# A hybrid attention block on one core: output projection reachable from attention's tail, first q and k by halves, shared transfer time in the planner

## The chip, the core and the metric

The kernel runs on one NeuronCore of a Trainium2 chip. TensorE (PE in the profile) multiplies into PSUM; VectorE (DVE), ScalarE (ACT) and GpSimd (POOL) work elementwise, and the queue of SyncE (SP) issues nearly all transfers. The engines run side by side; each takes its own instructions strictly in the order in which they were written. The metric is the device time of one execution in microseconds (us); lower is better. Before: 1434.74 us, the median of three runs (1434.43 to 1435.29).

## The reference

One layer over 1024 tokens of width 1024, all float32, each sub-layer between RMS norms with a residual:

- Token mixing: one projection of the normed input gives q, k and v of 16 heads of 64. Eight heads are "fox" heads: causal softmax attention with a cumulated log forget gate as bias. Eight are "chunk" heads: attention over the own chunk of 64 and the eight before it, with a relative-position bias. Each group's output is RMS-normed over its 512 columns, the two are joined, and `y @ w_out` follows (the output projection).
- Cross-attention of four heads of 256 into 256 memory tokens: projections `w_mq`, `w_mk`, `w_mv`, `w_mo`.
- An MLP of hidden size 4096 with a squared ReLU.

## The kernel before

**Arithmetic.** A product in float32 is made of three faster ones: each operand is split into a high and a low part (`hi`, `lo`), and `mm3` (lines 195 to 197) adds hi·hi, hi·lo and lo·hi in one PSUM bank. A weight block of 128x1024 comes by a transfer into one of three `wraw` buffers, ACT writes its high part (line 499), DVE or POOL its low part (line 505), and then the buffer is free for the next block. For q, k and v the block is also scaled: ACT sums its squares (line 462), PE adds them over the partitions (`nq`, line 472), POOL scales, ACT and POOL split.

**Stages.** A prologue written by hand norms the input and makes v of the first heads. The attention phase follows, up to about 517 us of the trace: for eight pairs of heads (chunk pairs 0 and 1, fox pairs 0 to 3, chunk pairs 2 and 3) the projections q and k (and v from the fifth pair on), scores (`sc..g` for chunk, `sf..g` for fox heads, two banks), softmax by DVE, ACT and POOL, transposes of the probabilities (`ptr`, line 795, split into `phl` by ACT, line 805, and DVE, lines 801 and 803), and products with v (`pv`, lines 840 to 843, read out into `o`, which goes to memory tensors `od`). Beside them run the memory projections `mk` and `mv`. The second phase holds the output projection `yw` (four 512x512 quarters for each of two head groups g = 0, 1; quarters by the half th of the tokens and the half nh of the columns), the queries of the cross-attention (`mq`), that attention itself (`ms`, `mtr`, `mo`), and its output projection (`ym`). From about 840 us on the MLP follows, written by hand.

**What sets the order.** In the attention phase and the second phase a planner, the class `Flow`, writes the instructions. It steps through generators ("streams"); each step of a stream is a few matmuls with a cost and a condition, and at every moment the first stream in the list whose condition holds places its step on PE. The last stream of the list is the filler: projections that need nothing of the attention chain (`filler_steps` in the attention phase, `second_filler` in the second). Work for DVE, ACT, POOL and the transfer queue is put into lists (`flow.put`, `flow.load`) with a planned earliest time, a cost and a level; when the planned engine is free, the entry of the lowest level that may start is written next. A transfer's result is planned to be there a fixed time after its issue. All these times are the planner's own; on the chip only the resulting order and the data count.

**Around the end of attention.** `Outputs` loads the finished fox-head outputs back (`oin`), four blocks for each half th of the tokens; ACT scales them into `yT_hi`, DVE writes `yT_lo`, ACT squares them (line 1146), DVE adds the squares up into `sq` (line 1124), and PE sums `sq` over the partitions (`ssh`, line 1164), which gives the norm factor `rs` of that half. The first `yw` matmul of the second phase needs `yT` and `rs` of half 0 and the first two blocks of `w_out`. The blocks of `w_out` come through the same three `wraw` buffers, behind the eight blocks of `w_mv`. In the profile's names `whiwo` and `whimv` are high parts of such blocks; `vm_hi` and `vm_lo` read the `mv` products out of PSUM.

The planner's list of the attention phase ends with the rows

```
flow.run([scale_steps(), value_steps(), turn_steps(), score_steps(), side_steps(), rstd_steps(0),
          filler_steps(keep)])
```

Of the kernel before, what the change touches and what calls it, by code (L numbers as in the profile page):

```python
# [20 lines left out]
ALU = mybir.AluOpType  # L21
# [36 lines left out]
class Flow:  # L58
# [4 lines left out]
    def __init__(self):  # L63
        self.now = self.end = 0.0
# [12 lines left out]
    def load(self, at, call, then=None, took=4.5, level=0):  # L77
        self.put("D", at, 0.55, call, then and (lambda end: then(end + took)), level)
# [59 lines left out]
def build(ctx, tc, nc, out, t):  # L138
# [265 lines left out]
    class Stock:  # L404
# [126 lines left out]
        def pump(self):  # L531

            while self.to_load:
# [13 lines left out]
                flow.put("D", flow.now, 0.55, lambda: None, lambda at, k=key: seen.__setitem__(("raw", k), at + 4.2))  # L547
# [37 lines left out]
    def split(key, at):  # L585
# [9 lines left out]
        flow.put("G", at, 1.15, lambda: stock.scale(key), lambda end: flow.put("S", end, 1.06, lambda: stock.hi(key), low, 2), 2)  # L595
# [44 lines left out]
    class Biases:  # L640
# [5 lines left out]
        def pump(self):  # L646
            while self.left and free["bias"].ready():
# [245 lines left out]
    def project_steps(what, n, part):  # L893
# [7 lines left out]
        for th in range(2):  # L901
# [31 lines left out]
            for a, (own, oth) in enumerate(HALVES):  # L933
# [14 lines left out]
                else:  # L948
# [16 lines left out]
    def side_steps():  # L965
# [24 lines left out]
        for k in range(0, KC, 2):  # L990
# [17 lines left out]
            flow.put("S", flow.end, 0.6, lambda src=src, dh=dh: nc.scalar.activation(dh, src, AF.Copy), lo, 1)  # L1008
# [89 lines left out]
    class Outputs:  # L1098
# [182 lines left out]
    def norm_steps():  # L1281
# [9 lines left out]
        def scales():  # L1291
# [9 lines left out]
            ("G", 0.7, lambda: nc.gpsimd.tensor_tensor(sw1, sw1, mhalf[:, 0:1], op=ALU.pow)), ("V", 1.1, scales)])))  # L1301
# [97 lines left out]
    def close_row(nm, n, at, dst, gnext, then):  # L1399
# [1712 lines left out]
```

## Time and profile before

| | before |
|---|---|
| median of 3 runs | 1434.74 us |
| the profiled execution, its own time | 1436.12 us |
| its span, first to last instruction | 1434.3 us |
| PE, DVE, ACT, POOL busy | 98%, 81%, 69%, 32% |
| granted TensorE clock, mean over the span | 0.994 |
| transfers | 295.72 MB, mean 206 GB/s |

Busy shares are means over stages. PE is busy nearly always, so the places that count are the few where PE stands still or runs at a lower clock. Three views tell them: the list of waits gives who ended PE's idle times, the timeline of an engine gives each instruction with the idle time before it in brackets, and the table by stretches gives the granted clock (PEclk, 1.00 is full speed). A matmul's printed duration is longer than its share of PE's time, since matmuls overlap; the distance from start to start is what one costs.

### The profile page before, as it was taken

The page shows a single profiled execution, that of the slowest core. Times are in us where ns is not written, and L with a number is a line of the kernel's source. Part 1 is how long each engine was busy: PE and PEld are TensorE (multiplying, and loading weights), DVE is VectorE, ACT ScalarE, POOL GpSimd, SP SyncE. Part 2 cuts the span into 40 slices and gives each one's busy share as a digit, 9 for nine tenths or more (in the row PEclk, how much of TensorE's full clock was granted, in tenths as well). Part 3 has the DMA queues.
Part 4 walks back from the last instruction along what each step waited for, and adds up shares of the span by engine and source line. Part 5 has one row for each costly group of instructions (what it writes and reads, how often), then busy time and mean ns, then how long its engine had stood idle before and what let it go on. Part 6 is the DMA issues. An engine that isn't in the chain of part 4 may idle for free.

```text
span 1434.3 us, 22534 instructions
## 1 busy us (share of the span) xinstructions
PE 1400.8 (98%) x7681; PEld 922.4 (64%) x7681; DVE 1156.0 (81%) x1863; ACT 989.1 (69%) x1688; POOL 454.8 (32%) x615
## 2 busy tenths in 40 slices
PE   8999999999999989999999999999999999999998
PEld 8746666666668868887888864444444445666653
DVE  7888776867777863779887978677998987899998
ACT  6678878888778844798465645786776657665654
POOL 2467768787645400121021531002223100000003
PEclk9999999999999989999999999999999999999999
DMA  7143465445436677471314656976888998686885
GB/s 281 49 132 91 142 187 170 121 148 142 128 106 167 203 223 275 169 292 38 111 59 133 205 177 220 339 256 219 290 287 290 347 366 306 235 307 225 308 304 205
DMA packets 118802, 295.72 MB, mean 206 GB/s; under 512 B 13448, under 2 KB 31888, under 8 KB 118688
## 3 DMA queue, kind: packets, MB, share of 16 engines
q1 hardware_dynamic: 118544, 294.03, 61.3%
q8 instruction: 60, 0.98, 0.3%
q14 instruction: 54, 0.44, 0.1%
q10 hardware_dynamic: 144, 0.26, 0.1%
HBM read 220.26 MB, written 65.59 MB: 199 GB/s over the span
## 4 chain that ended last, share of the span: by engine, by line
PE 71%; DVE 11%; ACT 6%; issue 5%; DMA 3%; POOL 2%; SPq 0%; DVEq 0%; ACTq 0%; POOLq 0%
PE ptr L795 4%; PE fx L195 3%; PE fx L196 3%; PE fx L197 3%; PE yw L195 2%; PE yw L196 2%; PE yw L197 2%; PE pv L840 2%; PE mq L196 2%; PE mq L197 2%; PE mq L195 2%; PE px L197 2%; PE px L196 2%; PE px L195 2%; PE k L195 1%
## 5 line engine op out<-in xcount | busy, mean ns | idle before, releaser
L805 ACT ACTIVATE phl<-ptr 128x512 f16<-128x512 f32 (+3 forms) x152 | 80.4, 537 | 41.3 <-PE ptr L795 39.5
L2879 POOL TENSOR_SCALAR rf<-sf 128x1 f32<-128x1 f32 x7 | 5.8, 825 | 280.3 <-ACT jf L2858 280.0
L2574 POOL TENSOR_TENSOR sc<-wf,wf 128x512 f32<-128x512 f32 x8 | 11.2, 1398 | 173.0 <-DMA wf<-in_w_ff 109.2
L1734 POOL TENSOR_SCALAR mp<-mp,mst 128x256 f32<-128x256 f32 x32 | 22.6, 709 | 127.0 <-DVE mst L1733 104.1
L803 DVE TENSOR_TENSOR phl<-ptr,phl 128x384 fp32r<-128x384 f32 (+1 forms) x76 | 46.3, 616 | 19.2 <-ACT phl L805 18.6
L801 DVE SCALAR_TENSOR_TENSOR phl<-ptr,phl 128x384 f16<-128x384 f32 (+1 forms) x76 | 46.4, 616 | 16.5 <-ACT phl L805 15.5
L840 PE MATMUL pv<-phl,vs 128*128 128x512 f32 (+1 forms) x152 | 53.0, 431 | 1.0 <-DVE phl L803 1.0
L2723 ACT ACTIVATE vhif<-ra,fsc 128x1024 f16<-128x1024 f32 x34 | 38.9, 1143 | 20.8 <-PE fx L197 12.6
L2725 DVE SCALAR_TENSOR_TENSOR vhif<-ra,fsc,vhif 128x1024 f16<-128x1024 f32 x34 | 43.5, 1279 | 11.2 <-ACT vhif L2723 10.9
L2723 ACT ACTIVATE whif<-ra,fsc 128x1024 f16<-128x1024 f32 x34 | 38.8, 1142 | 19.3 <-PE fx L197 10.3
L195 PE MATMUL yw<-whiwo,yT_hi 128*128 128x512 f32 x128 | 51.8, 404 | 0.0
L196 PE MATMUL yw<-wlowo,yT_hi 128*128 128x512 f32 x128 | 51.1, 399 | 0.0
L197 PE MATMUL yw<-whiwo,yT_lo 128*128 128x512 f32 x128 | 51.0, 399 | 0.0
L196 PE MATMUL q<-hF_lo,wq 128*128 128x512 f16 x128 | 48.5, 379 | 1.8 <-DVE hF_lo L2235 1.8
L195 PE MATMUL fx<-vlof,vhif 128*128 128x512 f16 x128 | 48.5, 379 | 0.8 <-DVE yc L2930 0.8
L195 PE MATMUL k<-hF_hi,wk 128*128 128x512 f16 x128 | 49.2, 384 | 0.0
L195 PE MATMUL q<-hF_hi,wq 128*128 128x512 f16 x128 | 48.9, 382 | 0.0
L196 PE MATMUL k<-hF_lo,wk 128*128 128x512 f16 x128 | 48.8, 381 | 0.0
L2725 DVE SCALAR_TENSOR_TENSOR whif<-ra,fsc,whif 128x1024 f16<-128x1024 f32 x34 | 43.5, 1279 | 6.5 <-ACT whif L2723 6.4
L197 PE MATMUL k<-hF_hi,wk 128*128 128x512 f16 x128 | 48.6, 380 | 0.0
L197 PE MATMUL q<-hF_hi,wq 128*128 128x512 f16 x128 | 48.5, 379 | 0.0
L195 PE MATMUL fx<-wlof,whif 128*128 128x512 f16 x128 | 48.5, 379 | 0.0
(855 smaller groups left out, 5350.5 us busy)
## 6 DMA issues: line engine op xcount, KB each, us to landing
wg<-in_w_ff SPq DMA_DIRECT2D x48, 512.0 KB, 5.3
ra<-gd SPq DMA_DIRECT2D x40, 512.0 KB, 4.8
wf<-in_w_ff SPq DMA_DIRECT2D x38, 512.0 KB, 4.5
wn<-in_w_ff SPq DMA_DIRECT2D x32, 512.0 KB, 4.8
w2n<-in_w_ff SPq DMA_DIRECT2D x32, 512.0 KB, 6.5
wi<-in_w_ff2q SPq DMA_DIRECT2D x28, 512.0 KB, 5.6
gd<-s SPq DMA_DIRECT2D x32, 256.0 KB, 6.0
gd<-g SPq DMA_DIRECT2D x19, 256.0 KB, 4.5
```

Source lines behind the costliest of these rows:

```text
L195: nc.tensor.matmul(ps, lh, rh, start=start, stop=False, skip_group_check=more)
L196: nc.tensor.matmul(ps, lh, rl, start=False, stop=False, skip_group_check=more)
L197: nc.tensor.matmul(ps, ll, rh, start=False, stop=stop, skip_group_check=more)
L795: nc.tensor.transpose(tr[:, m, :], sp[:, k * P:(k + 1) * P], ident)
L801: flow.put("V", at, 0.75, lambda: nc.vector.scalar_tensor_tensor(pl[:, live, :], tr[:, live, :], 2.0 ** 14, ph[:, live, :], op0=ALU.mult, ...
L803: if ph.dtype == F16 else nc.vector.tensor_sub(pl[:, live, :], tr[:, live, :], f(ph[:, live, :])), done)
L805: flow.put("S", flow.end, 0.6, lambda ph=ph, tr=tr, live=live: nc.scalar.activation(ph[:, live, :], tr[:, live, :], AF.Copy, scale=2.0 ** ...
L840: nc.tensor.matmul(pv[:, :, qs_, :], v, hl[:, :, hs, :], start=c == 0 and turn == 0, stop=last)
L1734: mul = lambda st=st, pr=pr: nc.gpsimd.tensor_scalar(pr, pr, st[:, 2:3], 1.0, op0=ALU.mult, op1=ALU.mult)
L2574: eng.tensor_sub(sc[:, k1], r0[:, k0], r1[:, k0])
L2723: nc.scalar.activation(ah, ra, AF.Copy, scale=su)
L2725: nc.vector.scalar_tensor_tensor(al, ra, su, ah, op0=ALU.mult, op1=ALU.subtract)
```

## The change

No instruction is added or removed in what is computed; the order changes from the first projections to the end of the second phase, and some transfers start elsewhere. The MLP's part is the same. Five edits:

1. **The output projection's stream is built before the attention phase** and given to its planner run as a stream after all others (`last=tail`); the run still ends when the other streams are empty, and the second phase goes on with the same stream.
2. **`Outputs` loads half 0 of the fox outputs once all q, k and v projections are placed** (and nine u4 buffers are free) instead of once all scores are placed; half 1 waits for the scores as before.
3. **The first pair's projections go by halves of the tokens**: q of half 0, k of half 0, q of half 1, k of half 1, where it was q, q, k, k.
4. **The planner counts shared transfer time**: `land` adds up the bytes at 310 KB a planned us, and a load is planned to be there at the later of its fixed time and the end of that sum. The copies between partitions of k are counted at 3.6 instead of 2.3.
5. **Other levels** for some 25 entries (an example is shown), and other starts and paces of three background streams: sums of squares of MLP weights (`Norms`: start 80 instead of 60; in the second phase three spare buffers instead of four), differences of query weights (`QuerySums`: start 100, pace 12 instead of 20, 18).

```diff
-        self.put("D", at, 0.55, call, then and (lambda end: then(end + took)), level)
+        self.put("D", at, 0.55, call, lambda end: self.land(end, took, then), level)
+
+    def land(self, end, took, then):
+        size = {2.2: 64, 2.5: 256, 3: 512, 3.5: 256, 3.6: 128, 4.2: 512, 4.5: 512, 6.0: 256, 7.5: 256}[took]
+        self.moved = max(self.moved, end + 1.5) + size / 310.0
+        if then:
+            then(max(end + took, self.moved + 0.6))
...
-    def run(self, streams, more=lambda: False):
-        heads = [[g, next(g, None)] for g in streams]
-        idle = 0
-        while any(h[1] for h in heads) or more():
+    def run(self, streams, more=lambda: False, last=None):
+        heads = [g if isinstance(g, list) else [g, next(g, None)] for g in streams]
+        needed, idle = list(heads), 0
+        if last:
+            heads.append(last)
+        while any(h[1] for h in needed) or more():
...
-                "G", end, 1.3, lambda: stock.lo(key, nc.gpsimd, 1), last, 2), 2)
+                "G", end, 1.3, lambda: stock.lo(key, nc.gpsimd, 1), last, 1), 2)
...
-                if not (there(("od", g), "scored") and free["u4"].ready(7) and (g == 0 or ("w", 1) in ys)):
+                late = there("scored")
+                if not (there(("od", g), "scored" if th or g else "projected") and
+                        free["u4"].ready(7 if late else 9) and (g == 0 or ("w", 1) in ys)):
...
-        START, PACE = 20.0, 18.0
+        START, PACE = 100.0, 12.0
...
             part = all_of(("qk", n), 12)
+            if n == 0:
+                for th in range(2):
+                    for what in "qk":
+                        yield from project_steps(what, n, part, (th,))
+                continue
...
+        seen["projected"] = flow.end
         yield from memory_steps(keep)
+
+    steps = second_filler()
+    tail = [steps, next(steps)]
...
-                  filler_steps(keep)])
+                  filler_steps(keep)], last=tail)
...
-                  norm_steps(), second_filler()], lambda: stock.to_load or stock.to_split)
+                  norm_steps(), tail], lambda: stock.to_load or stock.to_split)
```

How this moves instructions is shown at three places; numbers behind a name tell its instances apart, and in the changed file line numbers stand 9 to 12 higher.

**ACT at the end of attention.** Before (`whiwo_0_0`, `whiwo_0_1`: the two blocks of the first column half; `whiwo_1_0`: the first block of the second column half; `rs_6784`: norm factor of half 0):

```order
L1143 ACTIVATE yT_hi_6516<-oin_6521,gcol 128x512 x2
L1146 ACTIVATE oin_6520<-oin_6520 128x512
L1146 ACTIVATE oin_6521<-oin_6521 128x512 x2
L499 ACTIVATE whiwo_0_0_6808<-wrawwo_0_0_6752 128x1024
L499 ACTIVATE whiwo_1_0_6895<-wrawwo_1_0_6775 128x1024
L1086 ACTIVATE vm_hi_6572<-mv_6718 128x512
L499 ACTIVATE whiwo_0_1_6825<-wrawwo_0_1_6773 128x1024
L1086 ACTIVATE vm_hi_6573<-mv_6736 128x512
L1235 ACTIVATE wn_6811,wsq<-wn_6811 128x1024
L1458 ACTIVATE yw_6868<-yw_6867,rs_6784 128x512
```

With the change:

```order
L1155 ACTIVATE yT_hi_6579<-oin_6584,gcol 128x512
L1158 ACTIVATE oin_6584<-oin_6584 128x512 x2
L1096 ACTIVATE vm_hi_6471<-mv_6681 128x512
L508 ACTIVATE whiwo_0_1_6807<-wrawwo_0_1_6679 128x1024
L870 ACTIVATE o_6815<-pv_6764,wus 64x256
L1096 ACTIVATE vm_hi_6472<-mv_6692 128x512
L1470 ACTIVATE yw_6817<-yw_6816,rs_6555 128x512
L1247 ACTIVATE wn_6828,wsq<-wn_6828 128x1024
L508 ACTIVATE whiwo_1_0_6901<-wrawwo_1_0_6730 128x1024
L1470 ACTIVATE yw_6818<-yw_6849,rs_6555 128x512
```

`whiwo_1_0` stood ahead of both `vm_hi` and of `whiwo_0_1`; it now stands behind the first read-out of `yw`. `whiwo_0_0` stands nine rows above the first one shown.

**PE at the same place.** Before, the last `mv` matmuls, then the sum for half 1 (`ssh_6832`), then the output projection:

```order
L197 MATMUL mv_6736<-whimv_3_6748,mT_lo_5564 128x512
L1164 MATMUL ssh_6832<-o_81,sq_6519 128x1 x4
L1274 MATMUL top<-ident,wsq 128x128
L195 MATMUL yw_6867<-whiwo_0_0_6808,yT_hi_6508 128x512
L196 MATMUL yw_6867<-wlowo_0_0_6809,yT_hi_6508 128x512
```

With the change (the sum for half 0 stands 187 rows above):

```order
L206 MATMUL mv_6692<-whimv_3_6699,mT_lo_5470 128x512
L851 MATMUL pv_6764<-phl_6776,vs_71_5323 128x256
L204 MATMUL yw_6816<-whiwo_0_0_6715,yT_hi_5741 128x512
L204 MATMUL yw_6816<-whiwo_0_1_6807,yT_hi_5742 128x512
L205 MATMUL yw_6816<-wlowo_0_1_6808,yT_hi_5742 128x512
L206 MATMUL yw_6849<-whiwo_0_0_6715,yT_lo_5743 128x512
L1176 MATMUL ssh_6855<-o_81,sq_6582 128x1 x4
L1286 MATMUL top<-ident,wsq 128x128
```

Rows between these that differ in one name alone are left out: 15 `yw` matmuls now stand ahead of the sum for half 1. The last product of the attention stands right before them, where 42 `mv` matmuls had stood behind it.

**PE in chunk pair 1 (about 170 us of the trace).** Before, from one transpose group (`ptr_2134`) to the product that reads its split copy (`phl_2135`):

```order
L795 MATMUL ptr_2134<-ident,spc2g_1941 128x128
L840 MATMUL pv_2148<-phl_2105,vs_1_196 128x512
L840 MATMUL pv_2148<-phl_2105,vs_1_196 128x2x128
L795 MATMUL ptr_2154<-ident,spc2g_1941 128x128
L721 MATMUL sc3g_2165<-kd_1250,qs_1123 128x384
L722 MATMUL sc3g_2165<-kl_1251,qs_1123 128x384
L721 MATMUL sc3g_2168<-kd_1250,qs_1123 128x256
L722 MATMUL sc3g_2168<-kl_1251,qs_1123 128x256
L840 MATMUL pv_2148<-phl_2135,vs_2_197 128x512 x2
```

With the change, the same group (`ptr_2108`) and product (`phl_2109`):

```order
L804 MATMUL ptr_2108<-ident,spc2g_1888 128x128
L204 MATMUL q_1_2004<-hF_hi_699,wq_1191 128x512
L205 MATMUL q_1_2004<-hF_lo_701,wq_1191 128x512
L849 MATMUL pv_2128<-phl_2080,vs_1_196 128x512
L849 MATMUL pv_2128<-phl_2080,vs_1_196 128x2x128
L804 MATMUL ptr_2133<-ident,spc2g_1888 128x128
L730 MATMUL sc3g_2140<-kd_1232,qs_1115 128x384
L731 MATMUL sc3g_2140<-kl_1233,qs_1115 128x384
L730 MATMUL sc3g_2145<-kd_1232,qs_1115 128x256
L731 MATMUL sc3g_2145<-kl_1233,qs_1115 128x256
L849 MATMUL pv_2128<-phl_2109,vs_2_197 128x512 x2
```

Repeats are left out here too: the group's `ptr` rows are four, the next group's three, and six `q` matmuls (two `mm3`) now stand between the two groups, where none stood.

More of the change, by code (lines that the diff above doesn't have):

```diff
@@ L63, in __init__ @@
     def __init__(self):
-        self.now = self.end = 0.0
+        self.now = self.end = self.moved = 0.0
         self.free = dict.fromkeys(("V", "S", "G", "D"), 0.0)
@@ L546, in pump @@
                 self.load()
-                flow.put("D", flow.now, 0.55, lambda: None, lambda at, k=key: seen.__setitem__(("raw", k), at + 4.2))
+                flow.put("D", flow.now, 0.55, lambda: None, lambda at, k=key: flow.land(at, 4.2, mark(("raw", k))))
             while self.to_split and there(("raw", self.to_split[0])):
@@ L891, in all_of, with project_steps @@
         return one
-    def project_steps(what, n, part):
+    def project_steps(what, n, part, halves=range(2)):
         kind, pr = ORDER[n]
         u = 3 if what == "v" else 2
-        for th in range(2):
+        for th in halves:
             cs = slice(th * HT, (th + 1) * HT)
@@ L955, in then @@
                     def then(at, lo=lo, last=last, copy=copy, d=d, l=l):
-                        flow.load(at, lambda: copy(d), part, 2.3)
+                        flow.load(at, lambda: copy(d), part, 3.6)
                         flow.put("V", at, 0.75, lo, lambda end: (last(end), flow.load(
-                            end, lambda: copy(l), part, 2.3)), 1)
+                            end, lambda: copy(l), part, 3.6)), 1)
                     flow.put("S", flow.end, 0.7, hi, then, 1)
-        stock.done((what, n))
+        if 1 in halves:
+            stock.done((what, n))
     vt = {}
@@ L1006, in lo @@
                          lambda end: (free["tr"].give(end), seen.__setitem__(("mT", k), end)), 1)
[L1008 removed]
+            flow.put("S", flow.end, 0.6, lambda src=src, dh=dh: nc.scalar.activation(dh, src, AF.Copy), lo, 0)
         for _ in range(2):
@@ L1429, in wait @@
             if ("xt", nm, n) in seen:
-                flow.put("V", max(end, seen["xt", nm, n]), 1.3, add, store, 1)
+                flow.put("V", max(end, seen["xt", nm, n]), 1.3, add, store, 0)
             else:
                 flow.put("G", end + 0.5, 0.0, lambda: None, wait)
-        flow.put("G", at, 1.9, lambda: root(0, ss[:, 0:1], ss[:, 1:2]), wait, 1)
+        flow.put("G", at, 1.9, lambda: root(0, ss[:, 0:1], ss[:, 1:2]), wait, 0)
     def mix_steps(g):
@@ L1458, in mix_steps @@
                     flow.put("S", flow.end, 0.63, lambda yc=yc, ps=ps, r=r: nc.scalar.activation(
-                        yc, ps, AF.Copy, scale=r), free["mm"].give)
+                        yc, ps, AF.Copy, scale=r), free["mm"].give, 1)
                 else:
@@ L1467, in rest @@
                                   ("V", 0.7, lambda: nc.vector.tensor_tensor(yc, yc, gains["mix"][:, cs], op=ALU.mult))]
-                        flow.chain(at, parts_, (lambda end: close_row("w", n, end, x1d, "mem", mixed(n))) if nh else None, 1)
-                    flow.put("V", flow.end, 0.7, out, rest)
+                        flow.chain(at, parts_, (lambda end: close_row("w", n, end, x1d, "mem", mixed(n))) if nh else None, 5)
+                    flow.put("V", flow.end, 0.7, out, rest, 0)
             if th == 1:
@@ L1513, in lo @@
                     flow.put("V", at, 0.7, lambda: nc.vector.tensor_sub(dl, src, dh),
-                             lambda end: (free[bk].give(end), seen.__setitem__(key, end)))
-                flow.put("S", flow.end, 0.6, lambda src=src, dh=dh: nc.scalar.activation(dh, src, AF.Copy), lo)
+                             lambda end: (free[bk].give(end), seen.__setitem__(key, end)), 2)
+                flow.put("S", flow.end, 0.6, lambda src=src, dh=dh: nc.scalar.activation(dh, src, AF.Copy), lo, 2)
         for _ in range(4):
@@ L1622, in split @@
                          lambda at, hi=hi, lo=lo, r=raw[i], then=then: flow.put(
-                             "V", at, 1.22, lambda: nc.vector.tensor_sub(lo, r, f(hi)), then, 0), 0 if n == "A22" else 1)
+                             "V", at, 1.22, lambda: nc.vector.tensor_sub(lo, r, f(hi)), then, 0), 0 if n == "A22" else 3)
     class Finals:
@@ L1839, in operand_parts @@
                               ("V", 0.42, lambda: nc.vector.tensor_sub(s4, halves[0], L))],
-                   lambda at: (gone(at), [parts_of[n, k](at) for n in ("S2", "S1", "S4")]), 0)
+                   lambda at: (gone(at), [parts_of[n, k](at) for n in ("S2", "S1", "S4")]), 2)
         block(1, lambda at: (gone(at), lows[h, 1](at)), 1)
@@ L1869, in memory_out_steps @@
                                  "V", at, 0.7, lambda: nc.vector.tensor_sub(ol, ps, f(oh)),
-                                 lambda end: (free["pv"].give(end), done(end))))
+                                 lambda end: (free["pv"].give(end), done(end)), 3), 2)
                 free["pt"].give(flow.end)
@@ L1928, in gained @@
             return lambda at: flow.chain(at, parts_, (lambda e: close_row(
-                "m", b + 2 * th, e, x2d, "ff", mark(("h3", b + 2 * th)))) if close else None, 1)
+                "m", b + 2 * th, e, x2d, "ff", mark(("h3", b + 2 * th)))) if close else None, 3)
         def add(dst, x, then, op=nc.vector.tensor_add):
```

26 lines of the change are left out of this document (13 added, 13 removed).

## The prediction

> **What bounds the kernel now.** The page's head comes first: PE is busy for 98% of the span, so time can only come from the places where PE waits or runs slowly.
>
> ```profile
> span 1434.3 us, 22534 instructions
> PE 1400.8 (98%) x7681; PEld 922.4 (64%) x7681; DVE 1156.0 (81%) x1863; ACT 989.1 (69%) x1688; POOL 454.8 (32%) x615
> ```
>
> The list of waits (total us, times, longest) names the places; its longest single wait is at the end of attention:
>
> ```profile
> PE ssh L1164 <- DVE sq L1124: 5.7, 1, 5.7
> PE q L196 <- DVE hF_lo L2235: 1.8, 3, 0.8
> ```
>
> The timelines of SP, ACT, DVE and PE (start, duration, instruction, idle time before it and its releaser) say why:
>
> ```profile
> 512.59 0.38 SPq L450 DMA_DIRECT2D wrawwo<-in_w_out  x1
> 520.47 1.06 ACT L499 ACTIVATE whiwo<-wrawwo 128x1024 fp32r<-128x1024 f32 x1 [5.94 <-DMA wrawwo<-in_w_out]
> 521.44 0.58 ACT L1086 ACTIVATE vm_hi<-mv 128x512 fp32r<-128x512 f32 x1
> 521.91 1.05 ACT L499 ACTIVATE whiwo<-wrawwo 128x1024 fp32r<-128x1024 f32 x1
> 522.86 0.59 ACT L1086 ACTIVATE vm_hi<-mv 128x512 fp32r<-128x512 f32 x1
> 522.05 0.69 DVE L1087 TENSOR_TENSOR vm_lo<-mv,vm_hi 128x512 fp32r<-128x512 f32 x1 [5.76 <-ACT vm_hi L1086]
> 522.65 0.68 DVE L1124 TENSOR_TENSOR sq<-sq,oin 128x512 f32<-128x512 f32 x1
> 523.25 1.22 DVE L505 TENSOR_TENSOR wlowo<-wrawwo,whiwo 128x1024 fp32r<-128x1024 f32 x1
> 517.19 0.39 PE L196 MATMUL mv<-wlomv,mT_hi 128*128 128x512 f32 x1
> 517.42 0.39 PE L197 MATMUL mv<-whimv,mT_lo 128*128 128x512 f32 x1
> 523.48 1.84 PE L1164 MATMUL ssh<-o,sq 128*128 128x1 f32 x8 [5.68 <-DVE sq L1124]
> 525.29 0.77 PE L195 MATMUL yw<-whiwo,yT_hi 128*128 128x512 f32 x1
> 530.55 0.49 PE L195 MATMUL yw<-whiwo,yT_hi 128*128 128x512 f32 x1
> ```
>
> ACT stands for 5.94 us in front of `whiwo_1_0`, whose transfer, issued at 512.59, ends about 520.4: 7.8 us. `vm_hi` stands behind it on ACT, `vm_lo` behind that on DVE, and the last `sq` behind `vm_lo`; PE's `ssh` waits for that `sq`. Yet `whiwo_1_0` belongs to the second column half, which PE reaches 48 `yw` matmuls after the first one, 11 us at the 0.23 of the `mv` rows. So a block that nobody needed yet holds up all four engines. The table by stretches shows what follows, in the column PEclk:
>
> ```profile
> core 0: us, PE busy (x) PEld busy (x) DVE busy (x) ACT busy (x) POOL busy (x), PEclk, DMA share, GB/s
> 520.00:525.00 5.00, 1.52 (x8) 1.55 (x9) 2.42 (x3) 4.01 (x6) 0.00 (x0) 0.55 0.69 273
> 525.00:530.00 5.00, 5.00 (x14) 4.03 (x15) 2.70 (x8) 0.00 (x0) 1.53 (x2) 0.50 0.82 218
> 530.00:535.00 5.00, 5.00 (x22) 4.06 (x22) 2.44 (x3) 2.33 (x3) 0.00 (x0) 0.92 1.04 395
> 175.00:179.00 4.00, 3.60 (x15) 2.41 (x15) 3.71 (x13) 3.00 (x8) 3.56 (x5) 0.60 0.00 0
> ```
>
> The wait is followed by some ten us at half clock. The last row is a second, smaller such place, in chunk pair 1.
>
> **The change part by part.** No computing is added, so each term is a wait that goes, comes or moves. The sum is made against the profiled execution's 1436.12 us, which lies 1.4 above the median of 1434.74.
>
> *End of attention.* In the new order on ACT, `whiwo_1_0` stands behind `whiwo_0_1`, both `vm_hi` and the first read-out of `yw`. That removes the wait of 5.68. The half clock behind it goes too: the 12 `yw` from 525.29 to 530.55 took 5.26 instead of 12 x 0.23 (the distance of the `mv` rows) = 2.76, thus 2.5, and the eight `ssh` 1.84 instead of about half that, 0.9; together 3.4. What is late next? From the end of `mv_6681` on ACT does `vm_hi` (0.58) and `whiwo_0_1` (1.05), then DVE `wlowo_0_1` (1.22): 2.85. PE has 6 `mv`, 4 short `pv` and 7 `yw` to do meanwhile, 13 x 0.23 + 0.4 = 3.4. Then the second `vm_lo` and the last `sq` (0.69 + 0.68, with ACT's work ahead some 1.9) stand against the 8 `yw` that follow, 1.8. A wait of 0 to 0.8 may stay in front of `ssh`; I take 0.5. Term: -5.7 - 3.4 + 0.5 = **-8.6**; bounds 0 (the stall moves to another load) and -9.1.
>
> *Chunk pair 1.*
>
> ```profile
> 170.24 0.60 PE L795 MATMUL ptr<-ident,spc2g 128*128 128x128 f32 x4
> 173.33 0.73 PE L840 MATMUL pv<-phl,vs 128*128 128x512 f32 x2 [0.95 <-DVE phl L803]
> 174.71 0.44 PE L721 MATMUL sc3g<-kd,qs 128*128 128x384 f32 x1 [0.65 <-DVE mnc3g L725]
> 176.29 0.69 PE L721 MATMUL sc3g<-kd,qs 128*128 128x384 f32 x1 [0.40 <-DVE mnc3g L725]
> ```
>
> From the start of the last transpose (about 170.7) to the `pv` that reads its copy 2.65 us pass, and PE had 1.26 us of work. The six `q` matmuls that now stand in between add 6 x 0.215 = 1.29 (the `q` spacing shown below): 2.55, nearly all. The three waits sum to 2.0, and four us at clock 0.60 lose 1.6. Of these 3.6 I take **-2.9**; bounds 0 and -3.6.
>
> *Fox pair, 237 us.* One more wait of the same kind:
>
> ```profile
> 237.08 0.66 PE L795 MATMUL ptr<-ident,spf1g 128*128 128x128 f32 x4 [1.63 <-DVE phl L803]
> 131.55 0.45 PE L721 MATMUL sc1g<-kd,qs 128*128 128x384 f32 x1 [0.70 <-DVE mnc1g L725]
> ```
>
> Counted in the new order, the work in between grows from 1.33 to 2.53, by 1.2: **-1.3**, bounds 0 and -1.8. Conversely, at about 139 us four score groups of pair 0 now stand with only transposes between them. The nearest row is the one at 131.55, a wait of 0.70 for the same reason: **+0.8**, bounds 0 and +1.2.
>
> *First q and k.*
>
> ```profile
> 62.06 4.29 ACT L2234 ACTIVATE hF_hi<-xT 128x512 f16<-128x512 f32 x8
> 66.22 1.07 ACT L462 ACTIVATE wk<-wrawk 128x1024 f16<-128x1024 f32 x1
> 63.20 0.38 PE L195 MATMUL q<-hF_hi,wq 128*128 128x512 f16 x1
> 65.58 0.38 PE L196 MATMUL q<-hF_lo,wq 128*128 128x512 f16 x1 [0.76 <-DVE hF_lo L2235]
> 66.01 0.38 PE L195 MATMUL q<-hF_hi,wq 128*128 128x512 f16 x1
> 67.44 0.38 PE L472 MATMUL nq<-nq,o 128*128 128x1 f32 x2 [0.62 <-ACT wk L462]
> 70.39 1.17 PE L604 MATMUL ftr<-ident,fcol 128*8 128x128 f32 x8
> 72.68 0.38 PE L195 MATMUL k<-hF_hi,wk 128*128 128x512 f16 x1
> ```
>
> Two matmuls from 65.58 to 66.01: 0.215 each. The `q` of half 1, from 63.20 to 72.68, waits four times for half 1 of `hF` and the sum of squares of `wk`. Now the `k` of half 0, which needs neither, starts at 63.20. But PE executes in order, and after nine of its matmuls (65.14) comes `nq`, which ACT's L462 behind the eight `hF_hi` still releases at 67.44: one wait of 2.3. Behind it 15 matmuls (3.2) and `ftr` (1.0) end at 71.9 instead of 72.68: -0.75. If the longer idle time lowers the clock as at 175 us (1.6 to 1.7 lost) the edit costs 0.9; I take half a us for that: **-0.2**, bounds -0.75 and +0.9.
>
> On this the Trainium skill has a rule ("TensorE: Matmul & The Clock Gate", section "HAM oscillation — how this bites in real kernels"): no idle gaps above about 3.4 us on PE. By it the single 2.3 us would cost no clock, and the term would be -0.75. The trace agrees for the boundary, where 5.68 us came before the half clock; it differs at 175 us, where gaps of 0.95, 0.65 and 0.40 were followed by 0.60. So the measurement decides, and both ends stay.
>
> *Work moved into attention's tail.* Half 0 of the fox outputs is now scaled and squared there.
>
> ```profile
> 420.00:480.00 60.00, 59.77 (x458) 50.39 (x456) 45.47 (x108) 48.84 (x103) 33.04 (x50) 1.00 0.52 147
> L1143 ACT ACTIVATE yT_hi<-oin,gcol x8: 706/714/727, 494.0 to 509.7; 128x512 fp32r<-128x512 f32 x8
> L1144 DVE SCALAR_TENSOR_TENSOR yT_lo<-oin,gcol,yT_hi x8: 741/744/752, 494.8 to 512.2; 128x512 fp32r<-128x512 f32 x8
> ```
>
> Four blocks bring ACT 4 x 0.71 and four squares of 0.62, 5.3 us, and DVE 4 x 0.74 and three sums of 0.68, 5.0 us. In the 60 us of the row shown ACT would rise to 54.1 and DVE to 50.5: room, but less of it, and a `phl` that comes 0.5 late stops PE. The transfers (one MB, at a DMA share of 0.52) fit. For one or two such waits: **+1**, bounds 0 and +6.
>
> *Levels and shared transfer time in the second phase, paces.* The same instructions stand in other places; PE has no long wait there. I take **0**, bounds -1.9 (the nearest wait gone that is not named above, at this kernel's `q` sum of 1.8) and +3 (two waits of the 1.63 kind).
>
> Sum: -8.6 - 2.9 - 1.3 + 0.8 - 0.2 + 1 + 0 = -11.2, thus 1424.9 for the profiled execution and, 1.4 lower, **1423.5** for the median.
>
> **The rivals.**
> *A: attention's order gives nothing.* The covers in pairs 0 to 5 are counted, but each wait removed may come back a few rows later, since DVE (81% busy) is as late as before. For it: the new group of scores at 139 us. Against it: PE work between transpose and product grows nearly everywhere, not only at the two places. Without the terms -2.9, -1.3 and -0.2 the time is 1423.5 + 4.4 = 1427.9.
> *B: the boundary's stall moves.* ACT's next loads there, `whiwo_0_1` and `wn`, also wait for transfers; a load that lands 5 to 6 us late meets a cover of only 3.4 for the first. For it: the 7.8 us that `whiwo_1_0` took at a share of 0.69 to 0.82. Against it: the loads of half 0 stand some 30 issues of SP earlier, and the buffers come free earlier. The whole term lost: 1423.5 + 8.6 = 1432.1.
> *C, the slower side: ACT becomes the bound in attention's tail.* It decides when ACT has over about 57 of 60 us, where its `phl` copies come late one after the other. 23 such groups stand in the 60 us of the row; a wait of 0.65 each (the middle one of pair 1) is 15 us: 1438.5. For it: scaling entries now stand between the `phl` entries on ACT's queue. Against it: 54.1 is under 57.
> *D: the planner does not reach the new stream before attention ends.* The order shown excludes it: 15 `yw` stand ahead of `ssh`.
>
> **How the numbers follow.** Forecast 0.60, A 0.18, B 0.12, C 0.08, anything else 0.02. A measurement of this kernel tells about 0.2%, 2.9 us, from no change: the bounds are 1431.9 and 1437.6. The forecast and A are faster; B lies on the bound, two thirds of it within (0.08); C is slower. Half of the rest goes each way. That gives faster 0.82, same 0.09, slower 0.09. The range runs from 1416 (all lower ends of the two largest terms and of the second phase, -0.5 - 0.7 - 0.5 - 0.6 - 1.9 - 0.8 - 1 = -6, and a little more for waits not listed) to 1432, where B ends; C stays outside.
>
> **What would show it right or wrong.** In the new profile the list of waits should have no `ssh` wait above 1 us, the stretch behind the first `yw` a clock of 1.00, and ACT no `whiwo` idle time above 2 us. The three waits at 173 to 177 us should be gone together with the clock of 0.60; one wait for L462's sum of squares (line 471 there) of about 2.3 us should stand at 65 us, and `sc1g` waits near 139. A mean ACT share above 0.95 between 420 and 480 us, or a wait for `phl` there again and again, would make C right; an idle time of 5 us in front of `whiwo_0_1` or `wn` would make B right.

## The result, and the profile after

| | before | changed |
|---|---|---|
| median | 1434.59 us (1433.42 to 1435.29, 4 runs) | 1423.24 us (1422.69 to 1423.57, 4 runs) |
| the profiled execution, own time and span | 1436.12, 1434.3 us | 1422.69, 1420.7 us |
| granted TensorE clock, mean | 0.994 | 0.999 |

The ratio is 0.9921, 95% interval 0.9904 to 0.9939: 11.3 us less, where 11.2 were forecast (1423.5 us for 1423.24). A second set of five rounds on another occasion gave 1423.08 us and a ratio of 0.9924 (0.9913 to 0.9936). The two profiled executions lie 13.4 us apart, 2.1 more than the medians: the one of before lies 1.5 above its median, at a clock of 0.994, the one of the change 0.6 below. One of the 11 executions of the kernel of experiment 6 took 2051.97 us at a granted clock of 0.653; its ratio leaves it out.

The head of the page, and the longest entries of the list of waits of PE:

```profile
span 1420.7 us, 22525 instructions
PE 1394.8 (98%) x7681; PEld 917.3 (65%) x7681; DVE 1152.9 (81%) x1863; ACT 987.1 (69%) x1688; POOL 452.6 (32%) x615
```

```profile
PE nq L481 <- ACT wk L471: 2.6, 2, 2.1
...
PE tr_h2T L1555 <- ACT yw L1434: 1.6, 1, 1.6
```

The 5.7 us of `ssh` are gone from the list; what stands at its head now is the wait for the sum of squares of `wk`, and a new one at the turn to the second phase. The table by stretches at the end of attention and in chunk pair 1 (the heading as before):

```profile
515.00:520.00 5.00, 5.00 (x27) 4.21 (x27) 2.66 (x8) 3.53 (x5) 1.53 (x2) 1.00 0.58 193
520.00:525.00 5.00, 5.00 (x23) 4.09 (x22) 1.11 (x2) 1.38 (x2) 0.00 (x0) 1.00 0.99 365
175.00:179.00 4.00, 4.00 (x26) 2.82 (x25) 3.76 (x11) 3.93 (x10) 4.00 (x6) 1.00 0.32 115
```

PE is busy throughout, at full clock, where it had stood at 1.52 of 5 us and 0.50 to 0.55. The timelines of SP, ACT and PE at the same place:

```profile
491.57 0.55 SPq L459 DMA_DIRECT2D wrawwo<-in_w_out  x1
495.51 0.38 SPq L459 DMA_DIRECT2D wrawwo<-in_w_out  x1
500.18 2.61 SPq L459 DMA_DIRECT2D wrawwo<-in_w_out  x2
...
500.06 1.06 ACT L508 ACTIVATE whiwo<-wrawwo 128x1024 fp32r<-128x1024 f32 x1 [1.17 <-PE mv L206]
509.59 0.60 ACT L1096 ACTIVATE vm_hi<-mv 128x512 fp32r<-128x512 f32 x1 [0.21 <-PE mv L206]
510.08 1.05 ACT L508 ACTIVATE whiwo<-wrawwo 128x1024 fp32r<-128x1024 f32 x1
511.79 0.60 ACT L1096 ACTIVATE vm_hi<-mv 128x512 fp32r<-128x512 f32 x1
515.85 1.05 ACT L508 ACTIVATE whiwo<-wrawwo 128x1024 fp32r<-128x1024 f32 x1
...
514.65 0.95 PE L1176 MATMUL ssh<-o,sq 128*128 128x1 f32 x8
```

Three things changed at once: `whiwo_1_0` (515.85) stands behind both `vm_hi`; the first three blocks of `w_out` are issued 12 to 16 us earlier (491.57 to 500.18, where it was 507.92 to 512.59), so that none of the splits waits for its transfer; and 15 `yw` stand ahead of `ssh`. Experiments 1 and 2 take some of this apart, not all.

To see all places and not only the waits, the distance from each matmul's start to the next one's, less what its shape takes where nothing waits (0.228 us for 128x512 in f32, 0.216 in f16, and so on for the other shapes), is summed by stage; it holds waits and lost clock alike. `sc3g` are the scores of the second head of chunk pair 1. In us, from the traces of before, of the change, and of the change in the second set:

| stage | before | changed | again |
|---|---|---|---|
| start to the first scores | 10.9 | 12.2 | 11.6 |
| chunk pair 0, and pair 1 to the first `sc3g` | 3.5 | 3.2 | 2.9 |
| rest of chunk pair 1 | 5.0 | 0.7 | 0.7 |
| first fox heads | 2.7 | 1.1 | 2.3 |
| rest of attention, to the first `ssh` | 6.1 | 4.3 | 5.0 |
| first to third `ssh` (the boundary) | 10.4 | 1.4 | 1.4 |
| third `ssh` to the MLP | 6.8 | 8.0 | 8.0 |
| MLP | 8.6 | 9.5 | 9.2 |
| sum | 53.8 | 40.2 | 41.1 |

Each column is one execution. The two of the change differ by 1.2 in one stage, and the MLP, whose instructions are the same in all kernels, reads from 7.3 to 11.5 in this table and the next; so a difference of one us in a single stage is read only where several traces agree on it. The first `ssh` stands some 26 us earlier in the change, which moves the border between two stages: together "rest of attention" and "boundary" went from 16.5 to 5.7 and 6.4.

### The profile page after: what moved, and what is told of

Its sections match the earlier page's. It is cut to its first block, busy times and chain, and to the rows that moved or that the text cites. A ratio compares the mean times of both kernels' runs of the same rounds, so it can differ in the third digit from the quotient of the medians.

```text
span 1420.7 us, 22525 instructions
## 1 busy us (share of the span) xinstructions
PE 1394.8 (98%) x7681; PEld 917.3 (65%) x7681; DVE 1152.9 (81%) x1863; ACT 987.1 (69%) x1688; POOL 452.6 (32%) x615
## 4 chain that ended last, share of the span: by engine, by line
PE 75%; DVE 10%; ACT 6%; issue 5%; DMA 2%; POOL 1%; SPq 0%; DVEq 0%; ACTq 0%; POOLq 0%
PE ptr L804 4%; PE fx L204 3%; PE fx L206 3%; PE fx L205 3%; PE px L206 2%; PE px L204 2%; PE px L205 2%; PE pv L849 2%; PE yw L204 2%; PE yw L205 2%; PE yw L206 2%; PE mq L205 2%; PE mq L206 2%; PE mq L204 2%; PE k L204 2%
## 5 line engine op out<-in xcount | busy, mean ns | idle before, releaser
L2595 POOL TENSOR_TENSOR sc<-wf,wf 128x512 f32<-128x512 f32 x8 | 11.2, 1396 | 172.4 <-DMA wf<-in_w_ff 122.8
L2744 ACT ACTIVATE vhif<-ra,fsc 128x1024 f16<-128x1024 f32 x34 | 38.9, 1144 | 21.1 <-PE fx L206 10.2
L2746 DVE SCALAR_TENSOR_TENSOR vhif<-ra,fsc,vhif 128x1024 f16<-128x1024 f32 x34 | 43.5, 1281 | 10.6 <-ACT vhif L2744 10.3
L2744 ACT ACTIVATE whif<-ra,fsc 128x1024 f16<-128x1024 f32 x34 | 38.9, 1143 | 18.8 <-PE fx L206 10.3
L204 PE MATMUL k<-hF_hi,wk 128*128 128x512 f16 x128 | 49.0, 383 | 0.0
L204 PE MATMUL fx<-wlof,whif 128*128 128x512 f16 x128 | 48.5, 379 | 0.0
L205 PE MATMUL fx<-wlof,whif 128*128 128x512 f16 x128 | 48.5, 379 | 0.0
L206 PE MATMUL fx<-wlof,whif 128*128 128x512 f16 x128 | 48.5, 379 | 0.0
```

The costliest lines, as they stand in the source:

```text
L204: nc.tensor.matmul(ps, lh, rh, start=start, stop=False, skip_group_check=more)
L205: nc.tensor.matmul(ps, lh, rl, start=False, stop=False, skip_group_check=more)
L206: nc.tensor.matmul(ps, ll, rh, start=False, stop=stop, skip_group_check=more)
L2595: eng.tensor_sub(sc[:, k1], r0[:, k0], r1[:, k0])
L2744: nc.scalar.activation(ah, ra, AF.Copy, scale=su)
L2746: nc.vector.scalar_tensor_tensor(al, ra, su, ah, op0=ALU.mult, op1=ALU.subtract)
```

## The experiments

All medians, beside 1434.1 to 1434.4 us of the kernel before on the same occasion:

| kernel | us | ratio, 95% interval |
|---|---|---|
| before, one region (below) | 1428.08 | 0.9955 (0.994 to 0.997) |
| before with edits 1 and 2 | 1428.79 | 0.996 (0.9945 to 0.9974) |
| the change without edits 1 and 2 | 1443.04 | 1.0066 (1.0042 to 1.009) |
| the change without edit 3 | 1422.44, again 1422.32 | 0.992 (0.9906 to 0.9934), 0.9917 (0.9905 to 0.993) |
| the change without edit 4's shared transfer time | 1452.42 | 1.0124 (1.0108 to 1.0139) |
| the change without edit 5 | 1448.02 | 1.0099 (1.0085 to 1.0113) |
| the change, edit 5 undone in the second phase alone | 1431.15 | 0.9979 (0.9969 to 0.9988) |
| that, without 3, transfers of the second phase counted as before | 1439.46 | 1.0037 (1.0023 to 1.005) |
| without 3, and `h2` told 1.2 us later | 1430.99 | 0.998 (0.9971 to 0.9989) |
| the change, `nq` and `ftr` later | 1424.33 | 0.9933 (0.992 to 0.9945) |

And the sums by stage of some of them, in the order of the table above:

| kernel | start | pair 0 | pair 1 | first fox | rest | boundary | second | MLP |
|---|---|---|---|---|---|---|---|---|
| before, one region | 10.7 | 3.5 | 3.9 | 3.2 | 5.8 | 3.7 | 6.8 | 9.0 |
| before with 1, 2 | 10.2 | 3.5 | 3.9 | 2.7 | 9.1 | 1.4 | 6.7 | 7.3 |
| without 1, 2 | 12.3 | 3.2 | 0.7 | 1.8 | 7.2 | 10.6 | 19.4 | 11.5 |
| without 3 | 11.6 | 2.9 | 0.7 | 2.8 | 4.4 | 1.4 | 8.0 | 9.2 |
| without 4 | 12.0 | 4.1 | 8.9 | 3.2 | 9.2 | 1.9 | 20.5 | 9.9 |
| without 5 | 11.8 | 6.6 | 4.1 | 3.0 | 4.7 | 8.8 | 18.8 | 8.9 |
| 5 undone in the second phase | 11.8 | 3.3 | 0.7 | 1.8 | 4.5 | 1.4 | 18.6 | 8.4 |
| `h2` later, without 3 | 11.5 | 2.8 | 0.7 | 0.9 | 4.2 | 1.4 | 18.9 | 9.5 |

**1. ACT's order alone.** The account of the kernel before lacks something. The planner of the kernel before had written `whiwo_1_0` behind both `vm_hi`. But the attention phase and the second phase are two regions: within each an engine keeps the written order, while the framework settles how the end of one and the start of the other mix. It put the second region's first entry on ACT, `whiwo_1_0`, ahead of the first region's last three. The experiment makes one region of both:

```diff
-    with tc.manual_schedule():
+    whole = ExitStack()
+    whole.enter_context(tc.manual_schedule())
+    if True:
         xt, xloads = load_pair(0, 0, True)
...
-    with tc.manual_schedule():
+    if True:
         free["wq"].give(flow.now)
```

> The kernel before, with the two parts written by the planner put into one region in which each engine keeps the written order; the one thing that moves on PE, DVE, ACT and POOL is whiwo_1_0 on ACT, now behind both vm_hi and whiwo_0_1. Transfers are issued as before. Theory (what ACT's queue holds in front of vm_hi makes the boundary stall): the ssh wait falls from 5.7 to 1 to 2 us, the half clock behind it goes, 1425 to 1430 us. Rival (the late issue of the w_out blocks makes it, the order only says who shows the wait): whiwo_0_1 waits instead, 1433 to 1436 us.

Measured: 1428.08 us, 6.3 less than before, in the first theory's range. Waits of PE, the stretch that had half clock, and ACT somewhat later:

```profile
PE yw L195 <- ACT yw L1458: 1.3, 1, 1.3
PE ssh L1164 <- DVE sq L1124: 0.7, 1, 0.7
...
520.00:525.00 5.00, 5.00 (x23) 4.13 (x22) 2.84 (x5) 2.63 (x4) 0.45 (x1) 1.00 0.93 325
...
548.54 1.06 ACT L1235 ACTIVATE wn<-wn 128x1024 f32<-128x1024 f32 x1 [4.15 <-DMA wn<-in_w_ff]
```

The `ssh` wait is 0.7 and the clock full. The 1.3 in front of `yw` is the same fault in small: `wn`, weights of the MLP whose squares are needed much later, holds ACT for 4.15 us while read-outs of `yw` stand behind it. One flaw of the experiment: a load of gains that had stood ahead of `whiwo_1_0`'s on SP went behind it, so its transfer also began some 2 us earlier.

```profile
508.99 1.46 SPq L450 DMA_DIRECT2D wrawwo<-in_w_out  x2
518.23 1.06 ACT L1235 ACTIVATE wn<-wn 128x1024 f32<-128x1024 f32 x1 [0.64 <-DMA wn<-in_w_ff]
```

What that is worth can be estimated. `wn`, issued at 510.54 right behind `whiwo_1_0`'s block (510.08), was there at 518.23, after 7.7 us; the block itself, if it took its 7.8 us again, at 517.9. In the order of before, `ssh` ran 3.0 us after the block was there; that would be 520.9, a wait of about 4.0. So by this estimate the earlier transfer takes the wait from 5.7 to 4.0, and the order on ACT takes the rest.

**2. Early output alone.** Before, with `run(..., last=None)`, `tail` and the condition of `Outputs` of the change, and nothing else.

> The kernel before with edits 1 and 2 alone (output projection's stream in the attention run, half 0 of the fox outputs loaded once the projections are placed). Its order on ACT still has whiwo_1_0 ahead of whiwo_0_1 and of both vm_hi. Theory (ACT's queue): the stall at the boundary stays, within 2 us of its size, 1431 to 1436 us. Rival (the early output is what removes the stall): 1423 to 1428 us.

Measured: 1428.79 us. The theory missed; the stall is gone although `whiwo_1_0` still stands ahead of both `vm_hi`:

```profile
515.55 2.10 ACT L501 ACTIVATE whiwo<-wrawwo 128x1024 fp32r<-128x1024 f32 x2 [2.97 <-DMA wrawwo<-in_w_out]
518.88 0.60 ACT L1088 ACTIVATE vm_hi<-mv 128x512 fp32r<-128x512 f32 x1 [1.23 <-PE mv L199]
...
520.00:525.00 5.00, 5.00 (x24) 4.08 (x23) 2.99 (x9) 3.27 (x5) 0.55 (x1) 1.00 0.98 327
...
511.25 0.37 SPq L452 DMA_DIRECT2D wrawwo<-in_w_out  x1
```

ACT waits 2.97 us for the block here too (issued at 511.25, it was there after 4.3 us, not 7.8), but it is through before `mv` gives it the next read-out, for which it then waits 1.23. So a block that is not yet wanted does no harm on ACT's queue when it is there before the entry behind it can start. That the earlier transfers are enough by themselves is not shown, since edits 1 and 2 moved the other side too: the last `sq` now stands ahead of both `vm_lo` on DVE, and `ssh` ahead of the last 12 `mv` on PE.

```profile
514.32 0.68 DVE L1128 TENSOR_TENSOR sq<-sq,oin 128x512 f32<-128x512 f32 x1
516.39 0.95 PE L1168 MATMUL ssh<-o,sq 128*128 128x1 f32 x8
519.51 0.69 DVE L1089 TENSOR_TENSOR vm_lo<-mv,vm_hi 128x512 fp32r<-128x512 f32 x1 [0.61 <-ACT vm_hi L1088]
```

In this order a late `vm_hi` would not have reached `ssh` at all. The price is 3.0 us at the end of attention (9.1 against 6.1 in "rest"), where the waits for `phl` sum to 1.9 (0.4 before).

**3. The change without edits 1 and 2.** The five places of the diff that concern `last`, `tail`, `projected` and `late` are as before.

> The changed kernel without edits 1 and 2; attention is the same up to the tail, and no yw stands ahead of ssh. Its order on ACT has whiwo_1_0 behind both vm_hi. Theory (ACT's queue): no ssh wait above 2 us, 1423 to 1427 us. Rival (the early output carries the boundary's gain): a wait of 5 us or more with half clock behind it, 1430 to 1434 us.

Measured: 1443.04 us, 19.8 over the change (the profiled execution, on which its row of sums rests, took 1449.1). Neither number was right, but the rival's direction was. The order on ACT is good for `whiwo_1_0`; another load takes its part:

```profile
525.95 1.06 ACT L1243 ACTIVATE wn<-wn 128x1024 f32<-128x1024 f32 x1 [10.46 <-DMA wn<-in_w_ff]
...
PE yw L202 <- ACT yw L1466: 4.1, 1, 4.1
```

ACT stands 10.46 us in front of `wn`, and the read-outs of `yw` behind it. That is rival B of the prediction, in a kernel that lacks edits 1 and 2. Another 11 us go in the second phase.

**4. The levels of the second phase.** Of edit 5, what lies behind the third `ssh` undone, `SECOND` too; up to there nothing moves.

> The changed kernel with the old levels and paces in the second phase only; everything up to the second group of the output projection is the same. Theory (these levels earn nothing; the new waits at tr_h2T, 1.8 us, and mq, 0.9 us, are theirs): those waits go, 1421 to 1423 us. Rival (the levels save waits in the second phase): 1424 to 1428 us.

Measured: 1431.15 us, 7.9 over the change; the rival's direction was right, and the loss is 3 us above its range.

```profile
PE tr_h2T L1555 <- ACT yw L1434: 6.2, 1, 6.2
...
588.00:592.00 4.00, 4.00 (x19) 3.87 (x20) 0.15 (x1) 3.96 (x10) 0.54 (x1) 0.60 0.78 288
```

With the old levels the transposes `tr_h2T` stand behind 3 `yw` of the last quarter instead of 24; PE waits 6.2 us until ACT has normed the rows that they read (`yw`, L1434), and the clock falls to 0.60. The change has the same wait with 1.6.

**5. Is that wait the new accounting's doing?** As in 4, without edit 3, and in the second phase transfers counted as before (42 `yw` ahead of `tr_h2T`).

> The changed kernel without edit 3, with the old levels and paces in the second phase and, in that phase alone, transfers counted as before; 42 yw instead of 3 (with the old levels and the new accounting) or 24 (the change) stand between the third ssh and the tr_h2T transposes. Theory (the 6.3 us wait at tr_h2T with the old levels comes from the new accounting's place for them, and the levels only mend that): no such wait, 1420 to 1424 us. Rival (the levels are worth 8 us by themselves): 1429 to 1432 us.

Measured: 1439.46 us. The `tr_h2T` wait is gone as expected, and the time is worse all the same: other waits in the same phase (`mtr` for POOL 6.5 us in three, `ms` for DVE 3.5 in two, `mq` for ACT 1.9) with their clock, 24.7 us of excess in that stage. The theory fell.

**6. Telling the planner the truth about one row.**

```diff
-            seen["h2", n] = at
+            seen["h2", n] = at + 1.2
```

> The changed kernel without edit 3, and with the planner told 1.2 us more for a closed row of the output projection (key h2), so that six more yw stand ahead of the tr_h2T transposes. Theory (tr_h2T was placed 1.8 us too early): its wait falls from 1.8 to about 0.5, 1421 to 1422.5 us. Rival (the chain of the rows ends later with it, or a wait turns up behind): 1423 us or more.

Measured: 1430.99 us. The `tr_h2T` wait is gone, and later ones cost 11 us:

```profile
PE mtr L1767 <- POOL mp L1745: 3.1, 1, 3.1
PE mq L204 <- ACT S2q_h L1632: 2.6, 1, 2.6
...
645.50:649.50 4.00, 3.98 (x11) 2.87 (x12) 4.00 (x5) 2.87 (x6) 0.42 (x1) 0.50 0.00 0
```

Six `yw` moved, and from there on the planner made another plan. Five kernels (3, 4, 6, and 7 and 8 below) lose 18.6 to 20.5 us in the second phase, each at other waits, and 5 loses 24.7, where before and the change lose 6.8 and 8.0. What makes these two plans good was not found; it stays open.

**7. Without the shared transfer time.** `load` and the pump as before, no `land`, copies at 2.3.

> The changed kernel without edit 4's shared transfer time. Its order has the long stretch of scores and transposes without q matmuls in chunk pair 1 back, and whiwo_1_0 ahead of both vm_hi, but the w_out blocks are issued early. Theory (late issue and place on ACT's queue must come together for the stall): no ssh wait above 1.5 us, the three waits of pair 1 back with 3 to 5 us, 1425 to 1430 us. Rival (place on ACT's queue alone makes the stall): the ssh wait of 5 us and its half clock too, 1433 to 1438 us.

Measured: 1452.42 us. The boundary went as the theory said (1.9 us of excess, although `whiwo_1_0` stands ahead; `ssh` again stands ahead of the last 12 `mv`, so what experiment 2 leaves open this one leaves open too), pair 1 worse, and the second phase was not in the sum:

```profile
PE pv L842 <- DVE phl L805: 5.1, 2, 4.8
...
173.00:177.00 4.00, 3.68 (x13) 2.67 (x13) 1.66 (x5) 1.08 (x3) 0.00 (x0) 0.58 0.02 4
```

**8. Without edit 5 altogether.**

> The changed kernel without edit 5 (all levels, starts and paces as before). Its order has the long stretch of scores and transposes in chunk pair 1 as before, an early output, whiwo_1_0 behind both vm_hi, and 66 yw ahead of the tr_h2T transposes. Theory (the boundary's gain is that of edits 1, 2 and 4, pair 1's needs edit 5 too): boundary without a wait above 1.5 us, pair 1's three waits back with 4 to 5 us, 1426 to 1432 us. Rival (the levels are worth nothing): 1422 to 1425 us.

Measured: 1448.02 us, 16 over the top of the expectation. Pair 1 has its waits back (4.1), as said; the boundary does not stay clean (a block's low part is late for `yw`, 3.2), and the second phase waits 4.6 us for a block of `w_mq`.

```profile
PE mq L204 <- ACT whimq_B L508: 4.6, 1, 4.6
PE pv L849 <- DVE phl L812: 3.6, 2, 2.7
PE yw L205 <- DVE wlowo L514: 3.2, 1, 3.2
```

So pair 1's gain needs edits 4 and 5 together: without either, the `q` matmuls do not stand between its transposes.

**9. The halves.** The change with `q`, `q`, `k`, `k` in pair 0, in two sets, the second beside the change itself.

> The changed kernel without edit 3: q and k of the first pair whole again; everything from pair 1 on is in the same order as in the changed kernel. Theory (the halves only turn four short waits into one of the same sum): 1422.0 to 1424.5 us; the nq wait of 2.1 us goes, the q waits on hF_lo come back with 1.8. Rival (the halves earn their place): over 1425 us.

> The changed kernel once more, beside the three that follow on the same chip: 1422 to 1425 us; the measure for the next two.

> The changed kernel without edit 3, again beside the changed kernel. Theory (the halves cost a little: one wait of 2.1 us and two of ftr against four of 3.1 in sum): 0.3 to 1.3 us below the changed kernel of this job. Rival (the halves earn something): above it.

Measured: 1422.44 us; then 1423.08 with and 1422.32 without halves. Twice some 0.8 us less without them, with intervals that overlap (0.9905 to 0.993 and 0.9913 to 0.9936): by the medians edit 3 earns nothing, and the kernel without it, the lowest measured, is not set apart from the change. The traces say more. By the measure of the stage table, the stretch from the first `q` to the first scores holds 4.3 us in each of the seven profiled kernels with the halves and 3.3 or 3.4 in each of the seven without. So edit 3 costs about 1 us there.

**10. Why not.** The change with `nq` written when DVE's step that reads it is written (18 `k` matmuls ahead of it instead of 9), the `ftr` transposes likewise and 1.0 later in the plan. Of the rest of the program only some 40 rows of PE and a few of the other engines move.

> The changed kernel, halves included, with the nq matmul of wk written after 18 instead of 9 k matmuls (when DVE's step that reads it is written) and the ftr transposes 6 and 12 matmuls later; some 40 rows of PE and a few of the other engines stand elsewhere. Theory (the halves' gain is eaten by the place of nq and of ftr): the 2.3 us at nq and 0.9 at ftr fall to 1.4 or less in sum, 1420.5 to 1422.5 us. Rival (what is saved at the start is lost before the first scores or in pair 0): 1423 us or more.

Measured: 1424.33 us; the theory fell.

```profile
67.69 0.38 PE L482 MATMUL nq<-nq,o 128*128 128x1 f32 x2 [0.19 <-ACT wk L471]
70.24 0.60 PE L617 MATMUL ftr<-ident,fcol 128*8 128x128 f32 x4 [0.85 <-DVE wsc L485]
72.00 0.39 PE L204 MATMUL q<-hF_hi,wq 128*128 128x512 f16 x1 [1.16 <-DVE qs L959]
```

The `nq` wait fell from 2.13 to 0.19, and 0.85 came in front of `ftr` and 1.16 in front of the next `q`. Those two wait for DVE steps that stand behind six `hF_lo` on DVE's queue:

```profile
63.36 6.75 DVE L2262 TENSOR_TENSOR hF_lo<-xT,hF_hi 128x512 f16<-128x512 f32 x6
```

They end at 70.1 us here and at 70.3 in the change. So DVE sets the end of that stage, and PE's order only chooses which matmul shows it: the stretch from the first `q` to the first scores again holds 4.3 us. The 1.25 us above the change of the same occasion, within overlapping intervals, need not come from the start: this execution also waits 2.57 us for `mnf0g` at 201.80, where the two of the change waited 0 and 1.1.

## Why the prediction was right, point by point

The total was right, and so was the place of most of it. Sizes by the stage table, from the profiled executions:

- **The boundary, -8.6.** Measured -9.0 (10.4 to 1.4). No wait above 0.5 remained, and the clock is 1.00. The reason given, a block not yet wanted on ACT's queue, is borne out by experiment 1 (6.3 us, a smaller part of them by the block's own earlier transfer); but the prediction named it as the only reason. In experiment 2 the stall goes with the block still ahead. The change has the new order, the earlier blocks and the `yw` ahead of `ssh`; how the 9.0 divide among them stays open.
- **Chunk pair 1, -2.9.** Measured -4.3: the three waits and the clock of 0.60 are all gone, where 0.7 was left in the term for a `pv` that might still come late. But 1.1 of this is chance: the kernels of experiments 1 and 2 have the same three waits here (0.95, 0.65 and 0.40), kept the clock at 1.00 and read 3.9, so against them the gain is 3.2. From experiment 1:

```profile
175.00:179.00 4.00, 3.59 (x22) 2.33 (x20) 3.71 (x14) 3.55 (x8) 3.56 (x4) 1.00 0.00 0
```

- **Fox pair, -1.3; 139 us, +0.8.** The wait at 237 us is gone. The stage gained 1.6 in one execution of the change and 0.4 in another, where a wait of 1.1 for `mnf0g` stood at 200 us. At 139 us no wait came, and the 0.70 at 131 us went: the stage is 0.3 to 0.6 lower. There the term was wrong: two neighbouring groups of scores are not yet a wait.
- **First q and k, -0.2.** Measured +0.7 to +1.3 over the whole start, and +0.9 to +1.0 from the first `q` on (3.4 to 4.3). The single wait came as told, 2.13, in the first execution at full clock, but two more came in front of `ftr`:

```profile
67.84 0.38 PE L481 MATMUL nq<-nq,o 128*128 128x1 f32 x2 [2.13 <-ACT wk L471]
70.39 0.60 PE L613 MATMUL ftr<-ident,fcol 128*8 128x128 f32 x4 [0.20 <-DVE wsc L482]
71.36 0.60 PE L613 MATMUL ftr<-ident,fcol 128*8 128x128 f32 x4 [0.37 <-DVE wsc L482]
```

  The step that failed is "15 matmuls and `ftr` end at 71.9": they ended at 73.1 (six matmuls behind 71.80), since `ftr` stands behind a DVE step (`wsc`) that is through only after the six `hF_lo`. The half us taken for the clock did not show either way: in the second execution the same wait did lower the clock (0.57 in the 4 us behind it), and the stretch still held 4.3: the slower matmuls filled the time in which PE waited for DVE in the first.
- **Work moved into the tail, +1.** Measured -1.1 to -1.8, with the border of the stage moved as said above: no `phl` wait came. ACT rose to 51.7 of 60 us and DVE to 50.7 (forecast 54.1 and 50.5):

```profile
420.00:480.00 60.00, 59.74 (x472) 52.94 (x471) 50.73 (x116) 51.72 (x107) 33.04 (x48) 1.00 0.58 178
```

  So rival C's condition, 57 of 60, was never near.
- **Second phase, 0.** Measured +1.2: a new wait at `tr_h2T`, while the two at `mq` stayed about as long (0.7 and 0.6, before 1.5 in two).

```profile
587.53 1.64 PE L1555 MATMUL tr_h2T<-ident,yw 128*128 128x128 f32 x13 [1.65 <-ACT yw L1434]
```

  The zero was right for the change and wrong as a statement on its parts: undoing the levels alone costs 7.9 (experiment 4). The bound of +3 would have been far too narrow for the other six plans measured, which lose 10 us or more beyond this one.
- **MLP.** Not in the sum; +0.6 to +0.9. `px` waits for `wlo_a` 1.8 instead of 1.0, but the spread among kernels is as large, so whether the change does it is not shown.

Rival A (attention gives nothing) is out by pair 1. Rival B is out for the change, but its mechanism is what experiment 3 shows. The errors at the start, in the tail, in the second phase and in the MLP cancelled within 1 us; that the total agrees so well is in part luck. So is another part: the sum was made for the profiled execution, where it came out 2.2 too small (13.4 against 11.2), and the medians lie closer together than the two profiled executions by about as much.

## What to carry to other kernels

Where a long wait ends with one engine, look at what stands ahead on that engine's queue: here ACT stood 5.9, 4.2 and 10.5 us in three kernels for data that nobody wanted yet, with a read-out behind it that PE waited for. Take such an entry out of the way, or have its data there before what stands behind it can start. Edits to a planner's rules can't be priced one by one: all five together gave -0.8%, and with one group left out (1 and 2, 4, or 5) they gave +0.7 to +1.2%, so the order that comes out has to be read place by place, and the whole measured.

## What the runs showed of the hardware that was not expected

Whether a wait costs PE its clock depends on when it falls, not on its length alone. The wait of 2.13 us for `wk` left the clock at 1.00 in the first execution of the change. In the second, the same wait at the same place was followed by half clock. First the rows of the second execution, then those of the first:

```profile
67.28 0.38 PE L481 MATMUL nq<-nq,o 128*128 128x1 f32 x2 [2.13 <-ACT wk L471]
64.36:67.77 3.41, 1.28 (x8) 0.55 (x7) 3.41 (x4) 3.41 (x7) 2.48 (x3) 1.00 0.62 194
67.77:71.18 3.41, 3.41 (x10) 1.19 (x9) 3.31 (x6) 0.69 (x2) 2.25 (x7) 0.50 0.03 7
...
63.70:67.11 3.41, 2.02 (x10) 0.69 (x8) 3.41 (x4) 3.41 (x7) 2.48 (x3) 1.00 0.62 184
67.11:70.52 3.41, 2.47 (x13) 1.13 (x14) 3.38 (x5) 1.93 (x4) 2.57 (x7) 1.00 0.28 109
```

The stretches are chosen by the clock records in the traces: in each execution the granted clock changed only at times that lie a multiple of 3.413 us apart, with a start that differs from one execution to the next (before: 175.78, 179.19, 520.52, 530.76), and it stayed at half for 3.41, 6.83 or 10.24 us. At the boundary of the kernel before the half clock thus set in 3.0 us before the wait of 5.68 ended, and of its 10.24 us 7.3 lie behind the wait. In the 14 traces it fell 21 times between 25 us and PE's last matmul. In the step of 3.41 us before each fall, PE had stood idle for 1.61 to 3.41 us in all. At full clock, every step with 1.95 us or more of idle time was followed by a fall, none with less than 1.6, and in between both occur. So the 2.13 us that lie within one step cost the clock, and the same 2.13 us split into 1.4 and 0.7 do not. In two other kernels:

```profile
132.84 0.61 PE L849 MATMUL pv<-phl,vs 128*128 128x512 f32 x2 [2.71 <-DVE phl L812]
132.80:136.80 4.00, 3.65 (x19) 2.53 (x20) 3.68 (x13) 2.82 (x6) 1.87 (x3) 1.00 0.00 0
...
666.05 0.80 PE L204 MATMUL mq<-S2q_h,whimq_T 128*128 128x512 f32 x1 [2.58 <-ACT S2q_h L1632]
666.05:670.05 4.00, 3.34 (x7) 2.36 (x8) 3.67 (x4) 2.79 (x3) 0.00 (x0) 0.50 0.37 131
```

The 2.71 us are split into 1.93 and 0.78; of the 2.58 us 2.13 lie within one step. Short waits add up within a step: in pair 1 of the kernel before the clock fell at 175.78, after 0.95 and 0.65 us and before the third wait. A fall costs about 1.7 us for each 3.41 us at half clock in which PE has work. By these bounds, as an estimate, a single wait under 1.6 us among busy stretches keeps the clock, one over 3.9 us (twice 1.95) loses it, and what lies between is largely chance. The Trainium skill ("TensorE: Matmul & The Clock Gate", section "HAM oscillation — how this bites in real kernels") tells to keep idle gaps under about 3.4 us; here the clock fell behind single waits from 1.97 us up (experiment 4, at 651 us), so that bound does not keep it.
